# Sums of y's blocks on GpSimd beside the recurrence and memory attention, and both operands of the out-projection streamed, in a hybrid trunk layer on one core

## The chip, the cores and the metric

The kernel runs on one core of a Trainium2 chip. The metric is device time in microseconds (us), the median of several runs: 1556.83 us before the change, from 1556.57 to 1557.63 in three runs. Engines: TensorE (PE) multiplies matrices; VectorE (DVE), ScalarE (ACT) and GpSimd (POOL) work on elements; SyncE (SP) issues the DMAs of this kernel.

## The reference

One layer over 1024 rows of width 1024, in float32: a gated DeltaNet with 8 heads, a cross-attention of 4 heads over 256 memory tokens, one out-projection of both, and a SwiGLU FFN.

```python
def reference(x, mem, ...):
    h = x
    mem_n = rms_norm(mem, mem_norm)
    u = rms_norm(h, norm_pre_mix[layer])
    y_mix, q_mem = gdn_branch(u @ gdn_w_in[j], gdn_conv[j], gdn_a_log[j], gdn_dt_bias[j], gdn_out_norm[j])
    mem_k, mem_v = jnp.split(mem_n @ w_mem_kv[layer], 2, axis=-1)
    y_mem = memory_attention(q_mem, mem_k, mem_v)
    y = jnp.concatenate([y_mix, y_mem], axis=-1) @ w_out[layer]
    h = h + rms_norm(y, norm_post_mix[layer])
    f = swiglu(rms_norm(h, norm_pre_ffn[layer]), w_ffn_in[layer], w_ffn_out[layer])
    return h + rms_norm(f, norm_post_ffn[layer])

def memory_attention(q_mem, mem_k, mem_v):
    s = jnp.einsum("bhtd,bhmd->bhtm", q, k).astype(jnp.float32) * MEM_DH ** -0.5
    p = jax.nn.softmax(s, axis=-1).astype(v.dtype)
    return merge_heads(jnp.einsum("bhtm,bhmd->bhtd", p, v))
```

## The kernel before

All matrix products are float32 in three passes: each operand is split into a high part (a cast on ScalarE) and a low part (operand minus high part), and high x high, high x low and low x high are summed in PSUM. Who makes the low part depends on the place: here it is GpSimd for the left operand and VectorE for the right one.

The stages follow one another on TensorE, each filled up with products of the next: the input norm and transposes (to about 60 us); the recurrence over 8 heads in two halves of 512 rows, with the dense projections between its small products (to about 640); memory attention (to about 715); the out-projection (from 699 to about 854); the FFN's input products (to about 1317) and output products.

**Memory attention** has 16 units: 4 heads, two halves of the rows each, two units per half. `mem_q` projects a head's queries, `mem_scores` makes a unit's scores (psc), their maximum (mx), its negative scaled (nb), the exponential on ScalarE, its reciprocal sum (rc) and the product of both (pr). `mem_finish` takes the oldest unit from the list `pend`, transposes its probabilities (`mem_pt`, ptp) and, for the second unit of a half, multiplies by the values (`mem_pv`: pym, copied into ym and stored in y_d). Before the change a unit is finished after the scores of the next one, a lag of one. kvh and kvl are the halves of a head's keys and values.

**The out-projection** is y times w_out as 2 x 2 blocks. y has 12 heads of 128 columns: the first six columns of blocks (k = 0 to 5) belong to heads 0 to 5, the second six to heads 6 to 11, and its rows fall into two halves; these are A11, A12, A21, A22. Seven block products in Winograd's manner replace eight; `OPRODS` lists them for j = 0 to 6, and `o_prod(j)` runs one: six steps k, in each `o_operands(j, k)` loads and splits both operands (256 KB blocks), and `split_step` adds 4 x 3 matmuls, 72 for a product. The sums of w_out's blocks (T1 to T4) are made during the recurrence and stored in DRAM. The sums of y's blocks are made in the out-projection itself, in place in SBUF: in j = 1 A11 -= A21 (S3, VectorE) and A21 += A22 (S1, GpSimd), in j = 2 A22 -= A11 (S2, VectorE), in j = 3 A12 -= A22 (S4, VectorE), six adds each. So y's blocks stay in SBUF over the products, A11 and A12 in the pool `yp`, A21 and A22 in slots that belong to the FFN's weights (`free_slots`: names oB11h and so on in the trace). A22 itself is loaded again for j = 6, into the slots `raw` that the FFN's weights use too. `o_combine` adds a product's result to the output rows (hn<-acc).

Below, product 1 is j = 0, product 2 is j = 1, and so on. Beside the products VectorE and GpSimd also prepare the first weights of the FFN: multiply by a gain (L1057), sums of blocks (L1095), low parts (L93 for wlo<-raw, L1078 for plo and qlo).

Instructions go to an engine's queue in program order, except that `stage` and `issue_after` place a step behind a named instruction. An engine works its queue in order.

## Time and profile before

| | before |
|---|---|
| median of the runs shown | 1556.83 us |
| profiled execution | 1557.43 us |
| its span, first to last instruction | 1555.3 us |
| mean granted clock of TensorE | 0.986 |
| TensorE busy | 1477.7 us, 95% |
| VectorE busy | 1067.9 us, 69% |
| ScalarE busy | 680.4 us, 44% |
| GpSimd busy | 822.4 us, 53% |

The profile is of one execution; the times in its rows are measured from the span's start. The profiled execution took 2.1 us more than its span. A clock of 1.00 is TensorE's full speed (2.4 GHz), 0.50 its lower level (1.2 GHz).

### The profile page before, as it was taken

The page shows a single profiled execution, that of the slowest core. Times are in us where ns is not written, and L with a number is a line of the kernel's source. Part 1 is how long each engine was busy: PE and PEld are TensorE (multiplying, and loading weights), DVE is VectorE, ACT ScalarE, POOL GpSimd, SP SyncE. Part 2 cuts the span into 40 slices and gives each one's busy share as a digit, 9 for nine tenths or more (in the row PEclk, how much of TensorE's full clock was granted, in tenths as well). Part 3 has the DMA queues.
Part 4 walks back from the last instruction along what each step waited for, and adds up shares of the span by engine and source line. Part 5 has one row for each costly group of instructions (what it writes and reads, how often), then busy time and mean ns, then how long its engine had stood idle before and what let it go on. Part 6 is the DMA issues. An engine that isn't in the chain of part 4 may idle for free. (4 is left out here: it accounts for less than half of the span.)

```text
span 1555.3 us, 22654 instructions
## 1 busy us (share of the span) xinstructions
PE 1477.7 (95%) x8237; PEld 1180.3 (76%) x8237; DVE 1067.9 (69%) x1651; ACT 680.4 (44%) x1481; POOL 822.4 (53%) x705
## 2 busy tenths in 40 slices
PE   7999999999999999999898889999999999999996
PEld 5777777777777777887676668877887887778784
DVE  7565766656666757667977886666766766585967
ACT  7464445455454554345346532222222222544352
POOL 3543636464546544204755556666656565544455
PEclk9999999999999999999899899999999999999998
DMA  6411213122212220219334222222222324973334
GB/s 201 156 55 42 77 53 104 68 76 64 85 62 76 76 74 29 82 62 306 108 109 148 81 94 97 102 102 100 103 86 93 112 81 144 317 251 98 93 97 161
DMA packets 77554, 168.13 MB, mean 108 GB/s; under 512 B 10434, under 2 KB 12930, under 8 KB 77443
## 3 DMA queue, kind: packets, MB, share of 16 engines
q1 hardware_dynamic: 76720, 165.58, 31.9%
q8 instruction: 64, 1.05, 0.3%
q10 hardware_dynamic: 722, 1.12, 0.2%
q14 instruction: 48, 0.39, 0.1%
HBM read 124.42 MB, written 42.24 MB: 107 GB/s over the span
## 5 line engine op out<-in xcount | busy, mean ns | idle before, releaser
L246 PE MATMUL pj<-uhi,whi 128*128 128x512 f32 x496 | 215.7, 435 | 0.0
L93 POOL TENSOR_TENSOR wlo<-raw,whi 128x1024 fp32r<-128x1024 f32 x61 | 158.2, 2594 | 74.9 <-ACT whi L92 74.6
L246 PE MATMUL pj<-uhi,wlo 128*128 128x512 f32 x496 | 195.8, 395 | 0.0
L246 PE MATMUL pj<-ulo,whi 128*128 128x512 f32 x496 | 193.7, 391 | 0.0
L1292 POOL TENSOR_TENSOR wlo<-ar,whi 128x512 fp32r<-128x512 f32 x75 | 105.4, 1407 | 99.8 <-ACT whi L1291 99.8
L295 DVE SCALAR_TENSOR_TENSOR cv<-cb,convw_sb,cv 128x512 f32<-128x512 f32 x144 | 132.6, 921 | 24.0 <-ACT cv L290 23.3
L907 PE MATMUL fo<-wlo,whi 128*128 128x512 f32 x308 | 123.0, 399 | 9.4 <-DVE wlo L1292 9.2
L92 ACT CAST whi<-raw 128x1024 fp32r<-128x1024 f32 x66 | 69.6, 1055 | 119.2 <-DVE raw L1057 56.7
L908 PE MATMUL fo<-whi,wlo 128*128 128x512 f32 x308 | 120.6, 392 | 0.0
L906 PE MATMUL fo<-whi 128*128 128x512 f32 x308 | 118.4, 391 | 0.6 <-DVE c L854 0.6
L1095 DVE TENSOR_TENSOR raw<-raw 128x512 f32<-128x512 f32 x86 | 100.3, 1167 | 23.7 <-POOL wlo L93 13.7
L1292 DVE TENSOR_TENSOR wlo<-B,whi 128x512 fp32r<-128x512 f32 x75 | 80.9, 1081 | 45.9 <-ACT whi L1291 45.3
L246 PEld LDWEIGHTS pj<-uhi,wlo 128*128 128x128 f32 x496 | 93.1, 188 | 21.5 <-POOL wlo L93 0.2
L1057 DVE TENSOR_TENSOR raw<-raw,gcols_sb 128x1024 f32<-128x1024 f32 x44 | 64.1, 1457 | 57.9 <-DMA raw<-in_w_ffn_in 57.5
L246 PEld LDWEIGHTS pj<-ulo,whi 128*128 128x128 f32 x496 | 94.2, 190 | 10.8
L246 PEld LDWEIGHTS pj<-uhi,whi 128*128 128x128 f32 x496 | 94.0, 189 | 10.7 <-issue 0.2
L1291 ACT CAST whi<-ar 128x512 fp32r<-128x512 f32 x75 | 46.6, 621 | 113.1 <-POOL wlo L1292 75.4
L530 DVE TENSOR_TENSOR T<-pT,T 128x256 f16<-128x256 f32 x96 | 40.6, 423 | 59.5 <-PE pT L246 58.8
L907 PE MATMUL acc<-wlo,whi 128*128 128x512 f32 x168 | 68.7, 409 | 12.6 <-DVE wlo L891 12.6
L907 PEld LDWEIGHTS fo<-wlo,whi 128*128 128x128 f32 x308 | 58.2, 189 | 29.3 <-DVE wlo L1292 17.7
L1078 POOL TENSOR_TENSOR qlo<-raw,qhi 128x1024 fp32r<-128x1024 f32 x21 | 54.8, 2611 | 42.9 <-ACT qhi L1077 38.5
L517 DVE TENSOR_TENSOR zlev<-pz,lvmask_sb 128x256 f16<-128x256 f32 x96 | 40.4, 421 | 47.1 <-PE pz L246 47.0
(408 smaller groups left out, 4250.9 us busy)
## 6 DMA issues: line engine op xcount, KB each, us to landing
raw<-in_w_ffn_in SPq DMA_DIRECT2D x44, 512.0 KB, 3.3
raw<-in_w_in SPq DMA_DIRECT2D x36, 512.0 KB, 3.2
ar<-g_S SPq DMA_DIRECT2D x44, 256.0 KB, 2.6
B<-in_w_ffn_out SPq DMA_DIRECT2D x42, 256.0 KB, 4.6
g_A<-g SPq DMA_DIRECT2D x33, 256.0 KB, 2.0
ar<-g_A SPq DMA_DIRECT2D x29, 256.0 KB, 3.8
wsum<-in_w_out SPq DMA_DIRECT2D x24, 256.0 KB, 4.3
T_d<-wsum SPq DMA_DIRECT2D x24, 256.0 KB, 2.0
```

The costliest lines, as they stand in the source:

```text
L92: nc.scalar.copy(hi, raw)
L93: (lo_eng or nc.gpsimd).tensor_tensor(out=lo, in0=raw, in1=hi.bitcast(F32), op=ALU.subtract)
L246: ins = nc.tensor.matmul(*args, **kw)
L295: nc.vector.scalar_tensor_tensor(out=cf, in0=cb[:, c0:c0 + HF], scalar=w[:, j:j + 1], in1=cf, op0=ALU.mult, op1=ALU.add)
L906: nc.tensor.matmul(acc[n], hi[:, 0, ts_], hi[:, 1], start=first, stop=False)
L907: nc.tensor.matmul(acc[n], hi[:, 0, ts_], lo[:, 1], start=False, stop=False)
L908: return nc.tensor.matmul(acc[n], lo[:, 0, ts_], hi[:, 1], start=False, stop=last)
L1057: nc.vector.tensor_tensor(out=raw, in0=raw, in1=gcol[:, 1, :].unsqueeze(2).broadcast_to([P, ND, P]), op=ALU.mult)
L1078: nc.gpsimd.tensor_tensor(out=lo, in0=src, in1=hi.bitcast(F32), op=ALU.subtract)
L1095: nc.vector.tensor_tensor(out=o, in0=x, in1=y, op=op)
L1291: nc.scalar.copy(hi[:, i], src)
L1292: last_lo[i] = eng.tensor_tensor(out=lo[:, i], in0=src, in1=hi[:, i].bitcast(F32), op=ALU.subtract).ins
```

## The change

The six S3 = A11 - A21 are made on GpSimd in `post_y`, as each of heads 0 to 5 ends, and stored in DRAM (`s_d`). The other 18 sums (S2 = A22 - S3, S1 = A21 + A22, S4 = A12 - S2 for each k) are made on GpSimd by `y_sums`, in the loop over the units of memory attention: it loads A21 and S3, makes three sums and stores them. For k = 0 and 1 the second operands are heads 6 and 7, for k = 2 to 5 the fresh ym of a memory head. The out-projection holds no block: `o_operands` loads both operands of every step into the tags `oa` and `ob`, eight buffers each (the first two steps into `raw`). `o_sums`, `block` and `free_slots` are gone; j = 6 no longer uses `raw`. Memory attention finishes a unit after the scores of the second unit behind it, with three buffers for its small tiles.

```diff
@@ -46,8 +46,7 @@
 TFILL = (3, 4)
 W0 = 3
 POST = (1, 1, 2, 3)
-YP = ("A11", "A12")
-OPRODS = (("A11", "B11"), ("A12", "B21"), ("A22", "T2"), ("A21", "T1"), ("A12", "B22"), ("A11", "T3"),
+OPRODS = (("A11", "B11"), ("A12", "B21"), ("S2", "T2"), ("S1", "T1"), ("S4", "B22"), ("S3", "T3"),
           ("A22", "T4"))
 
 
@@ -67,6 +66,7 @@
     vm_d = [dram.tile([P, HF], F32, name=f"vm_d{i}") for i in range(2)]
     h_d = [dram.tile([P, D], F32, name=f"h_d{i}") for i in range(NT)]
     t_d = {n: [dram.tile([P, HF], F32, name=f"{n}_d{k}") for k in range(KH)] for n in ("T1", "T2", "T3", "T4")}
+    s_d = {n: [dram.tile([P, HF], F32, name=f"{n}_d{k}") for k in range(KH)] for n in ("S1", "S2", "S3", "S4")}
 
     def load_const(src, shape, dt, name, pool=None):
         t = (pool or const).tile(shape, dt, name=name)
@@ -631,13 +631,37 @@
         rstd_into(sc, rq2, 1.0 / (128.0 * 128.0), C4)
         nc.gpsimd.tensor_tensor(out=sc, in0=sc, in1=rq, op=ALU.mult)
         nc.gpsimd.tensor_scalar(out=sc, in0=sc, scalar1=128.0 ** -0.5, scalar2=1.0, op0=ALU.mult, op1=ALU.mult)
-        nc.gpsimd.tensor_tensor(out=os_, in0=os_, in1=bc(sc), op=ALU.mult)
+        st["os_ins"] = nc.gpsimd.tensor_tensor(out=os_, in0=os_, in1=bc(sc), op=ALU.mult).ins
 
     def post_y(h, hf, hd, st):
         pyt = transposes(st["os"], "pyt")
         y = hd["zs"][:, hf * HF:(hf + 1) * HF]
         nc.vector.scalar_tensor_tensor(out=y, in0=pyt, scalar=onorm, in1=y, op0=ALU.mult, op1=ALU.mult)
         nc.sync.dma_start(y_d[h][:, hf * HF:(hf + 1) * HF], y)
+        if hf == 1:
+            blocks = [hd["zs"][:, i * HF:(i + 1) * HF] for i in HO]
+            if h < KH:
+                t = pp.tile([P, HF], F32, tag="kvo", name="s3", bufs=3)
+                nc.gpsimd.tensor_tensor(out=t, in0=blocks[0], in1=blocks[1], op=ALU.subtract)
+                nc.sync.dma_start(s_d["S3"][h], t)
+            else:
+                ysums.append((h - KH, *blocks))
+
+    ysums = []
+
+    def y_sums(k, a12, a22):
+
+        s1 = hp.tile([P, HF], F32, tag="gr", name="s1", bufs=3)
+        nc.sync.dma_start(s1, y_d[k][:, HO[1] * HF:(HO[1] + 1) * HF])
+        s2 = hp.tile([P, HF], F32, tag="gr", name="s2", bufs=3)
+        nc.sync.dma_start(s2, s_d["S3"][k])
+        nc.gpsimd.tensor_tensor(out=s2, in0=a22, in1=s2, op=ALU.subtract)
+        nc.sync.dma_start(s_d["S2"][k], s2)
+        nc.gpsimd.tensor_tensor(out=s1, in0=s1, in1=a22, op=ALU.add)
+        nc.sync.dma_start(s_d["S1"][k], s1)
+        s4 = hp.tile([P, HF], F32, tag="gr", name="s4", bufs=3)
+        nc.gpsimd.tensor_tensor(out=s4, in0=a12, in1=s2, op=ALU.subtract)
+        nc.sync.dma_start(s_d["S4"][k], s4)
 
     def wo_block(i, j, k):
 
@@ -771,16 +795,16 @@
             nc.tensor.matmul(o, qh[:, t0:t0 + P], kvh[:, :NM], start=True, stop=False)
             nc.tensor.matmul(o, qh[:, t0:t0 + P], kvl[:, :NM], start=False, stop=False)
             nc.tensor.matmul(o, ql[:, t0:t0 + P], kvh[:, :NM], start=False, stop=True)
-        mx2 = small.tile([P, 2], F32, tag="mx2", name="mx2")
+        mx2 = small.tile([P, 2], F32, tag="mx2", name="mx2", bufs=3)
         nc.vector.tensor_reduce(out=mx2, in_=psc.rearrange("p (j m) -> p j m", j=2), axis=AX.X, op=ALU.max)
-        nb = small.tile([P, 2], F32, tag="nb", name="nb")
+        nb = small.tile([P, 2], F32, tag="nb", name="nb", bufs=3)
         nc.vector.tensor_scalar(out=nb, in0=mx2, scalar1=-MEM_SCALE, scalar2=None, op0=ALU.mult)
         pr = hp.tile([P, 2, NM], F32, tag="E", name="pr", bufs=3)
-        sm = small.tile([P, 2], F32, tag="sm", name="sm")
+        sm = small.tile([P, 2], F32, tag="sm", name="sm", bufs=3)
         for j in range(2):
             nc.scalar.activation(pr[:, j, :], psc[:, j * NM:(j + 1) * NM], AF.Exp,
                                  bias=nb[:, j:j + 1], scale=MEM_SCALE, accum_out=sm[:, j:j + 1])
-        rc = small.tile([P, 2], F32, tag="rc", name="rc")
+        rc = small.tile([P, 2], F32, tag="rc", name="rc", bufs=3)
         nc.vector.reciprocal(rc, sm)
         for j in range(2):
             nc.vector.tensor_scalar(out=pr[:, j, :], in0=pr[:, j, :], scalar1=rc[:, j:j + 1],
@@ -803,9 +827,15 @@
         for m in range(2):
             c0 = NM + m * P
             mm3(py, kvh[:, c0:c0 + P], kvl[:, c0:c0 + P], pth[m], ptl[m], m == 0, m == 1)
-        ym = hp.tile([P, HF], F32, tag="os", name="ym", bufs=2)
+        ym = hp.tile([P, HF], F32, tag=("os", "uf")[hm % 2], name="ym", bufs=2)
         nc.vector.tensor_copy(ym, py)
         nc.sync.dma_start(y_d[H + hm][:, hf * HF:(hf + 1) * HF], ym)
+        yms.append(ym)
+        if len(yms) == 2:
+            ysums.append((hm + H - KH, *yms))
+            yms.clear()
+
+    yms = []
 
     def mem_units():
         for hm in range(MH):
@@ -832,18 +862,22 @@
             with tc.issue_after(pj_ins[0]):
                 stage(post_y, ypend.pop(i))
         pend.append((hf, n2, cur, tiles, mem_scores(hf, n2, *cur)))
-        if len(pend) > 1:
+        if len(pend) > 2:
             mem_finish()
+        if i >= 4 and i % 2 == 0 and ysums:
+            with tc.issue_after(st[2 * H - 1]["os_ins"]):
+                y_sums(*ysums.pop(0))
     mem_finish()
+    mem_finish()
+    for job in ysums:
+        y_sums(*job)
     s1u.close()
-
 
 
 
 
     s2y = ExitStack()
     yp = s2y.enter_context(tc.tile_pool(name="yp", bufs=1, reuse_waits="tile"))
-    oblk = {}
 
     def load_row(pool, i):
         t = pool.tile([P, D], F32, name=f"grow{i}", bufs=1)
@@ -854,7 +888,9 @@
         return eng.tensor_tensor(out=out, in0=x, in1=y, op=op)
 
     def load_block(t, name, k):
-        if name[0] == "A":
+        if name[0] == "S":
+            src = s_d[name][k]
+        elif name[0] == "A":
             i, j = int(name[1]) - 1, int(name[2]) - 1
             src = y_d[k + KH * j][:, HO[i] * HF:(HO[i] + 1) * HF]
         else:
@@ -864,27 +900,14 @@
     def o_raw():
         return wp.tile([P, 2, HF], F32, tag="raw", name="raw", bufs=2)
 
-    def block(name, k):
-        if (name, k) not in oblk:
-            t = yp.tile([P, HF], F32, name=f"{name}_{k}", bufs=1) if name in YP else free_slots.pop(0)
-            oblk[name, k] = t
-            load_block(t, name, k)
-        return oblk[name, k]
-
     def o_operands(j, k):
-        an, bn = OPRODS[j]
-        first = j == 0 and k < 2
-        raw = o_raw() if j == 6 or first else None
-        if j == 2:
-
-            add(block("A22", k), block("A22", k), block("A11", k), op=ALU.subtract)
-        if raw is None:
-            srcs = [block(an, k)]
+        if j == 0 and k < 2:
+            raw = o_raw()
+            srcs = [raw[:, 0], raw[:, 1]]
         else:
-            srcs = [raw[:, 0]]
-            load_block(raw[:, 0], an, k)
-        srcs.append(raw[:, 1] if first else yp.tile([P, HF], F32, tag="ob", name="ob", bufs=OB))
-        load_block(srcs[1], bn, k)
+            srcs = [yp.tile([P, HF], F32, tag=t, name=t, bufs=OB) for t in ("oa", "ob")]
+        for src, name in zip(srcs, OPRODS[j]):
+            load_block(src, name, k)
         hi, lo = (wp.tile([P, 2, HF], F32R, tag="w" + c, name="w" + c, bufs=3) for c in ("hi", "lo"))
         for i, (src, eng) in enumerate(zip(srcs, (nc.gpsimd, nc.vector))):
             nc.scalar.copy(hi[:, i], src)
@@ -892,14 +915,6 @@
         return hi, lo
 
     last_lo = [None, None]
-
-    def o_sums(j, k):
-
-        if j == 1:
-            add(block("A11", k), block("A11", k), block("A21", k), op=ALU.subtract)
-            add(block("A21", k), block("A21", k), block("A22", k), nc.gpsimd)
-        elif j == 3:
-            add(block("A12", k), block("A12", k), block("A22", k), op=ALU.subtract)
 
     def split_step(acc, n, first, last, hi, lo):
         ts_ = slice(n * P, (n + 1) * P)
@@ -1010,7 +1025,6 @@
         for k in range(KH):
             hl = o_operands(j, k)
             with tc.issue_after(last_lo[0]), tc.issue_after(last_lo[1]):
-                o_sums(j, k)
                 if j and k < 4:
                     o_combine(j - 1, k, oprev[0][k])
                 if j >= 5:
@@ -1124,11 +1138,6 @@
     bp = s4.enter_context(tc.tile_pool(name="bp", bufs=1, side="right", reuse_waits="tile"))
     s2 = ExitStack()
     pt_ = s2.enter_context(tc.tile_pool(name="pt", bufs=2, side="right", reuse_waits="tile"))
-    free_slots = []
-    for pool, tags, n in ((bp, ("B11h", "B11l", "B21h", "B21l"), 4), (mp, ("phi", "plo", "qhi", "qlo"), 2)):
-        for tag in tags:
-            t = pool.tile([P, n, HF], F32, tag=tag, name="o" + tag, bufs=1)
-            free_slots += [t[:, i] for i in range(n)]
     x1, x2 = ([pt_.tile([P, D], F32, tag="hn", name="hn", bufs=8) for _ in range(4)] for _ in range(2))
     grow = {0: load_row(pt_, 0)}
     wx = s2y.enter_context(tc.tile_pool(name="wx", bufs=1, reuse_waits="tile"))
```

On VectorE, from the second product on (the numbers behind A_0 to A_5 and acc are those of tiles; A_0_8805 and its like are blocks A11, oB11h and its like blocks A21 and A22). Before:

```order
L854 TENSOR_TENSOR A_0_8805<-A_0_8805,oB11h 128x512
L891 TENSOR_TENSOR wlo<-ob,whi 128x512
L854 TENSOR_TENSOR A_1_8834<-A_1_8834,oB11h 128x512
L854 TENSOR_TENSOR oB11h<-oB11h,A_0_8805 128x512
L854 TENSOR_TENSOR A_2_8671<-A_2_8671,oB11l 128x512
L854 TENSOR_TENSOR oB11h<-oB11h,A_1_8834 128x512
L891 TENSOR_TENSOR wlo<-ob,whi 128x512
L854 TENSOR_TENSOR A_3_8693<-A_3_8693,oB11l 128x512
L854 TENSOR_TENSOR oB11l<-oB11l,A_2_8671 128x512
L854 TENSOR_TENSOR A_4_8715<-A_4_8715,oB21h 128x512
L854 TENSOR_TENSOR oB11l<-oB11l,A_3_8693 128x512
L891 TENSOR_TENSOR wlo<-ob,whi 128x512
```

After, from the second product's first low parts to the middle of the third (hn<-acc_8891 is the first sum with a result of product 2):

```order
L914 TENSOR_TENSOR wlo<-ob,whi 128x512 x7
L1071 TENSOR_TENSOR raw<-raw,gcols_sb 128x1024
L888 TENSOR_TENSOR hn<-acc_8891,hn 128x512
L914 TENSOR_TENSOR wlo<-ob,whi 128x512
L888 TENSOR_TENSOR hn<-acc_8892,hn 128x512
L1071 TENSOR_TENSOR raw<-raw,gcols_sb 128x1024
L1109 TENSOR_TENSOR raw<-raw 128x512
L914 TENSOR_TENSOR wlo<-ob,whi 128x512
L888 TENSOR_TENSOR hn<-acc_8893,hn 128x512
L1109 TENSOR_TENSOR raw<-raw 128x512
L1109 TENSOR_TENSOR s_9193<-raw 128x512
L1109 TENSOR_TENSOR raw<-raw,s_9193 128x512
```

The sums between the low parts are gone, and so are both multiplies between them (L1071, L1057 before): one stood in the second product and now stands at the start of the third, where the other one, the sums of FFN weights (L1109, L1095 before) and hn stood already.

On GpSimd, from the second product on, before (oB11h<-oB11h and its like are the sums S1; wlo<-A are low parts of the second product, wlo<-oB11h of the third):

```order
L891 TENSOR_TENSOR wlo<-A_0_8795,whi 128x512
L891 TENSOR_TENSOR wlo<-A_1_8824,whi 128x512
L891 TENSOR_TENSOR wlo<-A_2_8853,whi 128x512
L93 TENSOR_TENSOR wlo<-raw,whi 128x1024
L854 TENSOR_TENSOR oB11h<-oB11h 128x512
L891 TENSOR_TENSOR wlo<-A_3_8880,whi 128x512
L854 TENSOR_TENSOR oB11h<-oB11h 128x512
L891 TENSOR_TENSOR wlo<-A_4_8907,whi 128x512
L854 TENSOR_TENSOR oB11l<-oB11l 128x512 x2
L891 TENSOR_TENSOR wlo<-A_5_8933,whi 128x512
L854 TENSOR_TENSOR oB21h<-oB21h 128x512 x2
L891 TENSOR_TENSOR wlo<-oB11h,whi 128x512 x2
```

After, from the low parts of the first product's last three steps (the rows with s and ym are the last group of sums, for k = 5):

```order
L914 TENSOR_TENSOR wlo<-oa,whi 128x512 x3
L658 TENSOR_TENSOR s_8720<-ym,s_8720 128x512
L660 TENSOR_TENSOR s_8718<-s_8718,ym 128x512
L663 TENSOR_TENSOR s_8726<-ym,s_8720 128x512
L914 TENSOR_TENSOR wlo<-oa,whi 128x512 x8
L93 TENSOR_TENSOR wlo<-raw,whi 128x1024
L914 TENSOR_TENSOR wlo<-oa,whi 128x512 x2
L1092 TENSOR_TENSOR plo<-raw,phi 128x512
L1092 TENSOR_TENSOR plo<-s_9193,phi 128x512
L1092 TENSOR_TENSOR qlo<-raw,qhi 128x1024
L914 TENSOR_TENSOR wlo<-oa,whi 128x512 x16
```

The last group of sums stands between the low parts of the first and the second product, and L93 has moved behind eight low parts, which is into the third product, ahead of plo and qlo (L1078 before).

On GpSimd in the recurrence, after (L645 is the new S3, between the work of two heads; nothing else in these rows is new):

```order
L85 TENSOR_TENSOR rk<-rs,mhalf 128x4
L283 MEMSET cb 128x4
L645 TENSOR_TENSOR s_4510<-zs 128x512
L629 TENSOR_TENSOR rq_4533<-rq_4533,ss_4497 128x4
L83 TENSOR_SCALAR rs<-rq_4533 128x4
L85 TENSOR_TENSOR sc<-rs,mhalf 128x4
```

The subtraction stands behind a head's last small work and ahead of the next head's L629.

## Rows read from the trace of the kernel before

**Rows 1.** The page, busy time of each engine, share of the span, instructions.

```profile
PE 1477.7 (95%) x8237; PEld 1180.3 (76%) x8237; DVE 1067.9 (69%) x1651; ACT 680.4 (44%) x1481; POOL 822.4 (53%) x705
```

**Rows 2.** Windows: us, busy by engine, instructions; then clock, DMA share, GB/s.

```profile
640.00:720.00 80.00, 78.83 (x419) 63.17 (x418) 53.62 (x139) 42.05 (x129) 13.03 (x13) 1.00 0.36 120
726.00:750.00 24.00, 19.80 (x74) 14.97 (x74) 21.78 (x18) 8.76 (x16) 19.24 (x12) 0.86 0.66 228
750.00:774.00 24.00, 19.51 (x76) 14.73 (x75) 21.98 (x20) 11.40 (x23) 18.19 (x11) 0.93 0.38 121
790.00:806.00 16.00, 16.00 (x73) 13.23 (x72) 10.01 (x11) 7.56 (x14) 7.81 (x6) 1.00 0.34 99
806.00:830.00 24.00, 17.68 (x75) 13.53 (x74) 20.24 (x19) 13.53 (x27) 19.42 (x24) 1.00 0.43 155
```

**Rows 3.** TensorE's waits from 726 to 774: total us, times, longest.

```profile
PE acc L907 <- DVE wlo L891: 7.5, 4, 2.8
PE acc L908 <- POOL wlo L891: 1.2, 2, 0.6
```

**Rows 4.** Timeline of TensorE: start, duration, instruction, idle time before it.

```profile
750.17 0.39 PE L906 MATMUL acc<-whi 128*128 128x512 f32 x1
753.35 0.50 PE L907 MATMUL acc<-wlo,whi 128*128 128x512 f32 x1 [2.78 <-DVE wlo L891]
...
754.92 0.63 PE L906 MATMUL acc<-whi 128*128 128x512 f32 x1
...
757.48 0.48 PE L906 MATMUL acc<-whi 128*128 128x512 f32 x1
757.80 0.40 PE L907 MATMUL acc<-wlo,whi 128*128 128x512 f32 x1
758.03 0.39 PE L908 MATMUL acc<-whi,wlo 128*128 128x512 f32 x1
```

**Rows 5.** Timeline of VectorE in the second and third product.

```profile
736.05 1.77 DVE L854 TENSOR_TENSOR A<-A,oB11l 128x512 f32<-128x512 f32 x1
...
741.12 0.68 DVE L854 TENSOR_TENSOR A<-A,oB11l 128x512 f32<-128x512 f32 x1
...
751.54 1.75 DVE L891 TENSOR_TENSOR wlo<-ob,whi 128x512 fp32r<-128x512 f32 x1
```

**Rows 6.** Timeline of GpSimd in the first three products.

```profile
717.13 1.30 POOL L891 TENSOR_TENSOR wlo<-A,whi 128x512 fp32r<-128x512 f32 x1 [4.57 <-ACT whi L890]
...
737.23 1.75 POOL L891 TENSOR_TENSOR wlo<-A,whi 128x512 fp32r<-128x512 f32 x1
...
764.50 2.41 POOL L1078 TENSOR_TENSOR qlo<-raw,qhi 128x1024 fp32r<-128x1024 f32 x1
```

**Rows 7.** VectorE's groups, 726 to 774: count, busy us, mean ns, idle before.

```profile
L854 DVE TENSOR_TENSOR hn<-acc,hn 128x512 f32<-128x512 f32 x5 | 3.4, 678 | 0.0
L1057 DVE TENSOR_TENSOR raw<-raw,gcols_sb 128x1024 f32<-128x1024 f32 x2 | 2.4, 1211 | 0.0
...
L1095 DVE TENSOR_TENSOR raw<-raw,s 128x512 f32<-128x512 f32 x1 | 0.7, 695 | 0.0
```

**Rows 8.** VectorE's groups in memory attention, 640 to 726.

```profile
L777 DVE TENSOR_SCALAR nb<-mx 128x2 f32<-128x2 f32 x16 | 4.3, 276 | 0.0
...
L757 DVE TENSOR_TENSOR kvl<-kvr,kvh 128x512 fp32r<-128x512 f32 x3 | 2.0, 682 | 0.0
```

**Rows 9.** Timelines of VectorE and GpSimd at 711.

```profile
711.48 1.11 DVE L777 TENSOR_SCALAR nb<-mx 128x2 f32<-128x2 f32 x1
...
711.27 1.30 POOL L891 TENSOR_TENSOR wlo<-A,whi 128x512 fp32r<-128x512 f32 x1 [5.35 <-DVE mx L775]
```

**Rows 10.** The window with the most DMA traffic around the products.

```profile
720.00:740.00 20.00, 17.84 (x78) 14.12 (x76) 15.51 (x12) 10.88 (x19) 14.31 (x9) 1.00 0.94 334
```

**Rows 11.** Timeline of GpSimd in the recurrence.

```profile
395.07 0.64 POOL L484 TENSOR_SCALAR_AFFINE_SELECT at<-at 128x512 f32<-128x512 f32 x1 [2.86 <-DVE at L481]
```

## The prediction

> **What bounds the kernel now.** The page's busy times come first: TensorE works 1477.7 of 1555.3 us, VectorE 69%, GpSimd 53% [rows 1]. A gain has to come out of the 78 us that TensorE idles, or out of work at a low clock. Next, the windows: in memory attention TensorE is busy 78.83 of 80 us, in the fifth product 16.00 of 16; in products 2 and 3 it is busy 19.80 and 19.51 of 24 us, at granted clocks of 0.86 and 0.93 [rows 2]. A product is 72 matmuls. At the pace of 790 to 806 (73 records in 16 us, 0.219 us each, those cut by the edges counted in) 24 us would hold 109.5; the two windows hold 74 and 76. So product 2 loses 35.5 x 0.219 = 7.8 us and product 3 33.5 x 0.219 = 7.3. Product 6 (806 to 830, 75 records) loses about as much, but no sum stands there.
>
> The waits of these 48 us name VectorE's wlo (7.5 us) and GpSimd's (1.2) [rows 3]. What delays them is in the engines' own order. On VectorE an add of two SBUF tiles takes 0.68 us at 741.12 and 1.77 at 736.05 [rows 5]; GpSimd's multiplies of the same size take 1.30 at 717.13, with VectorE elsewhere, and 1.75 at 737.23 [rows 6]. At 733 to 741 both engines are full with sums and wlo, and each prolongs the other. VectorE's hn<-acc, with one operand from PSUM, keeps its 0.68 us through the same stretch [rows 7]. So it is not the number of sums alone that costs, but two-SBUF work of both engines at once: each has to wait out the other's instruction.
>
> **The change part by part.**
>
> *Sums leave products 2 and 3.* Gone are 12 VectorE adds and 6 GpSimd adds from product 2 and the start of 3, and 6 VectorE adds from product 4 (no loss there, so 0). Product 2 then holds no more than wlo of both engines, 6 x (0.68 + 1.30) = 11.9 us of two-SBUF work in 16.3, less than product 5, which also loses nothing: I take off its whole loss, -7.8. Product 3 opens with a wait: one matmul at 750.17, the next at 753.35, 3.18 us less a pace of 0.23, or 2.95 [rows 4], for the wlo that starts at 751.54 and takes 1.75 us, behind the last sum on VectorE [rows 5]. Behind that wait TensorE runs at the lower level (1.2 GHz): from 754.92 to 757.48 six matmuls take 0.427 each, just after 0.23 again; that is 1.2 us, and I add 0.4 for the matmuls on both sides of them, 1.6 [rows 4]. Both leave with the sums: -2.95 - 1.6 = -4.55. Removed together: -12.35.
>
> *What stays in product 3, and gets more.* Of its 7.3, 7.3 - 4.55 = 2.75 belong to the preparation of the FFN weights. The order shows that GpSimd's 128x1024 lo (L93), which stood in product 2, now stands in product 3 among the wlo, ahead of the two plo and the qlo, and VectorE's first multiply (L1057) moves from product 2 to the start of 3. They take 2.4, as the qlo of the same size does [rows 6], and 1.2 us [rows 7]. If they find room, 0; if all of it reaches TensorE, +3.6; I take half, +1.8, since product 3 is already the fuller one.
>
> *The 18 sums beside memory attention.* They are three GpSimd instructions for each k, some 1.3 us each, 4 to 5 us a group. GpSimd is nearly empty there (13.03 of 80 us [rows 2]), so their own time is hidden; the price is what they do to VectorE, busy 53.62 of these 80 us. The only neighbours in the trace: nb, a tiny VectorE operation, takes 1.11 us at 711.48 while a GpSimd wlo runs from 711.27 to 712.57 [rows 9], and 0.16 otherwise (the mean of 16, 276 ns, holds two such hits [rows 8]). A hit thus costs 1.11 - 0.16 = 0.95. Bounds: 0, if the lag of two covers all, to 18 x 0.95 = 17.1, if every sum hits a chain that TensorE waits for. TensorE waits for the softmax chain only after two more units, about 5 us each (16 units in 80 us), so hits on nb or pr vanish; not covered is the change of heads, where kvl and the copy into ym stand directly ahead of TensorE's next products [rows 8]. A group starts just after the second ym of a head, thus exactly there. Five groups with one hit each, some 0.6 of its 0.95 seen by TensorE: +3.0. That is nearer to the low end, since 5 of 18 sums are exposed.
>
> *The last group and the start of product 2.* On GpSimd the last three sums wait for the last ym, and all wlo of product 2 stand behind them. That ym ends at about 720.8 (before the change); three sums give 724.7 to 725.9 (1.30 to 1.7 each), the first wlo 726.0 to 727.6. Product 2's third matmul, which reads it, is due at 726.7. The wlo that follow need 1.3 to 1.75 per step of 2.7, so the delay doesn't return. From 0 to +4 (a later ym by the lag, contention on every instruction); taken +0.5.
>
> *S3 in the recurrence.* Six GpSimd subtractions of 1.3 us. GpSimd waits there for VectorE (2.86 us before the select at 395.07 [rows 11]). They are hidden in those waits; without this cover 6 x 1.3 = 7.8. Taken +0.5.
>
> *The lag of two.* It can give back no more than what memory attention loses: 80 - 78.83 = 1.2 [rows 2]. Bounds -1.2 and 0; taken half, -0.6. The extra buffers take no instruction.
>
> *Streamed operands.* A product now loads 12 blocks of 256 KB, 3.1 MB in 16.3 us or 193 GB/s; the core has moved 334 GB/s in 720 to 740 [rows 10], without a wait for a DMA in the products. On SP the stores of the last group stand ahead of product 3's first loads: free at about 726, wanted at about 740. 0. The second FFN load no longer waits for raw slots that product 7 held; that can only help products 6 and 7: 0 to -6, taken 0.
>
> The sum: -12.35 + 1.8 + 3.0 + 0.5 + 0.5 - 0.6 = -7.15. The profiled execution took 1557.43, which gives 1550.3; the median is 0.6 lower, so **1549.7 us**, 0.5% less.
>
> The Trainium skill, page "SBUF — State Buffer", section "Who interferes with whom", speaks against this change: VectorE and GpSimd share a port pair that one instruction holds to its end, two SBUF operands or VectorE's two-port modes (copy, tensor_scalar) take it, and one SBUF operand at most doesn't. The rows agree: 0.68 against 1.77 us for an add, 0.68 throughout for hn<-acc [rows 5, 7]. Its rule is rival A below.
>
> **The rivals.**
> *A. GpSimd's sums hold up VectorE in memory attention, slower (10%).* Mechanism: each sum runs against pr, nb, kvl; VectorE, two thirds busy, falls behind by one hit per sum, and the lag doesn't refill. For it: the hit at 711.48 [rows 9]. Against it: VectorE has 26 us of idle in the 80 [rows 2], 18 hits take 17. At full price 17.1 + 7.8 for the S3 hits instead of 3.5: 1549.7 + 21.4 = 1571. The break-even is 18 sums at 0.56 us seen by TensorE each (7.15 + 3.0 = 10.15 over 18); by this case the time is 1560 to 1571. By the page's rule, tensor_scalar pr would be hit as well, which makes this case's 17.1 and no more.
> *B. Product 3 stays as slow as it is (25%).* Without sums it still holds 6 x 1.98 = 11.9 us of wlo, and 2.4 (L93) + 2 x 1.3 (plo) + 2.4 (qlo) on GpSimd and 2 x 1.2 (L1057) + 4 x 0.69 (L1095) on VectorE [rows 6, 7]: 24.5 us of two-SBUF work in 16.3. If the two engines exclude each other fully, 8.2 us are lost, less what wlo's three buffers run ahead. For it: that sum, and that product 5, with 11.9, loses nothing. Against it: product 2 runs light, so product 3 starts some steps ahead. Loss 8.2 in place of 2.75 + 1.8: 1549.7 + 3.6 = 1553.3, and 1552 to 1554 with what the lead is worth and the start of product 2 costs.
> *C. Product 6 and what follows gain too (12%).* Product 6 loses 24 - 75 x 0.219 = 7.6 us [rows 2], through FFN weights prepared beside it. If those of the next k are loaded and multiplied in memory attention, half of it goes: 1549.7 - 5 = 1545. Against it: the order of VectorE's and GpSimd's rows from product 4 on is the old one.
> *D. Nothing comes of it (8%).* The streams are late: 42 loads and 24 new stores on one queue, and product 3 reads S2 that was stored 15 us earlier. The wait on VectorE becomes one for a DMA of about the same size: 1556 to 1557. Against it [rows 10].
>
> **How the numbers follow.** The forecast itself has 45%, its own range 1546 to 1552. B gives 1552 to 1554, C 1542 to 1546, D about 1557, A 1560 and more. A measurement here tells about 0.2%, 3.1 us, from no change: faster is below 1553.7. The forecast, C and two thirds of B lie there: 0.73; D and the rest of B are the same: 0.17; A is slower: 0.10. The range from 1540 to 1557 leaves out A and a little below C.
>
> **What would show it.** In the profile after: product 2 in about 16.5 us with TensorE's clock at 1.0 in it, no wait for VectorE's wlo above 1 us; product 3 in 20 to 21.5 us, with a wait for GpSimd's wlo behind L93 or qlo (at 24 B holds). VectorE's nb and kvl of 1 us and more beside s<-ym in memory attention, yet TensorE's gaps there some 3 us in sum (10 or more: A). First matmul of product 2 with no wait over 0.5 us. No wait for oa or ob anywhere. Wrong I'd be most easily in the 3.0 for memory attention and in product 3's rest.

## The result and the profile after

The changed kernel takes 1564.92 us (median of 9 runs, 1561.69 to 1566.86), the kernel before 1557.32 (9 runs, 1549.87 to 1562.69): ratio 1.0052, 95% interval 1.0031 to 1.0072. It is slower by half a per cent, and clear of the noise, where 0.5% less was forecast. The profiled execution took 1561.69, its span is 1559.9 us.

Executions of one and the same kernel differ by some 20 us (25 runs of the kernel before beside experiment 1 took 1547.71 to 1568.79). So the comparisons below go by single stretches of TensorE's order: the start of one named matmul to that of another, read from the timelines, one profiled execution of each kernel.

| stretch, us | before | after | difference |
|---|---|---|---|
| recurrence: first pkk of unit 3 to first pkk of unit 15 | 422.4 | 431.5 | +9.1 |
| rest of it, memory attention, product 1 | 123.6 | 129.2 | +5.6 |
| product 2 | 23.9 | 17.1 | -6.8 |
| product 3 | 23.6 | 23.4 | -0.2 |
| products 4 and 5 | 32.6 | 32.6 | 0.0 |
| products 6 and 7 | 47.4 | 45.7 | -1.7 |
| sum | 673.5 | 679.4 | +6.0 |

(pkk are the products of a unit's keys; a product runs from its first matmul to the next product's first, and the last row ends at the start of product 7's last matmul; differences and sum are from the unrounded numbers.) Busy times on the page after, against [rows 1]:

```profile
PE 1482.8 (95%) x8237; PEld 1177.5 (75%) x8237; DVE 1047.8 (67%) x1633; ACT 679.7 (44%) x1481; POOL 845.5 (54%) x723
```

VectorE has 18 instructions less and GpSimd 18 more, as planned; TensorE, with the same 8237 records, is busy 5.1 us longer, a first hint that its work itself has become slower somewhere. The windows that answer to [rows 2]: memory attention (the same 80 us from the span's start, though the work comes some 10 us later now), product 2, product 3, product 5, product 6.

```profile
640.00:720.00 80.00, 75.59 (x413) 60.66 (x412) 50.16 (x124) 35.66 (x112) 31.43 (x30) 1.00 0.46 151
742.00:759.00 17.00, 16.53 (x74) 13.36 (x73) 8.37 (x8) 9.27 (x17) 10.40 (x8) 1.00 0.97 340
759.00:783.00 24.00, 19.43 (x77) 14.64 (x76) 19.75 (x18) 11.68 (x25) 19.03 (x11) 0.93 0.63 204
799.00:815.00 16.00, 16.00 (x73) 13.23 (x72) 9.95 (x11) 7.57 (x14) 7.77 (x6) 1.00 0.61 197
815.00:840.00 25.00, 19.52 (x74) 14.38 (x73) 19.49 (x19) 14.60 (x27) 20.35 (x24) 0.94 0.56 189
```

Product 2 is cured: 17 us, clock 1.00, while DMA moves 340 GB/s. Product 3 is what it was, clock 0.93 and all.

**The recurrence.** TensorE's waits from unit 3 to unit 15, before and then after:

```profile
PE pc L246 <- DVE vn L597: 3.9, 13, 0.3
```

```profile
PE pc L246 <- DVE vn L597: 8.3, 18, 1.0
```

Five more waits of just under 1 us, one for each of the first five S3; the sixth, made at 599.5 near the end of the stretch, has none. The timeline of GpSimd after, at one of them, shows an S3 and what stands behind it:

```profile
382.03 1.29 POOL L645 TENSOR_TENSOR s<-zs 128x512 f32<-128x512 f32 x1 [9.72 <-DVE zs L639]
383.28 0.20 POOL L629 TENSOR_TENSOR rq<-rq,ss 128x4 f32<-128x4 f32 x1
...
387.37 1.04 POOL L457 TENSOR_TENSOR E<-gr,gc 128x512 f32<-128x512 f32 x1
388.36 1.49 POOL L634 TENSOR_TENSOR os<-os,sc 128x512 f32<-128x512 f32 x1
389.81 1.09 POOL L458 TENSOR_SCALAR_AFFINE_SELECT E<-E 128x512 f32<-128x512 f32 x1
```

The S3 hides in nothing: the 9.72 us ahead of it are its own wait for zs, and when zs comes, everything behind it is due. E ends at 390.9. The timelines of ScalarE (first before, then after), VectorE and TensorE carry it on:

```profile
384.50 0.63 ACT L469 ACTIVATE E<-E 128x512 f32<-128x512 f32 x1 [0.48 <-POOL E L458]
```

```profile
390.93 0.63 ACT L469 ACTIVATE E<-E 128x512 f32<-128x512 f32 x1 [1.77 <-POOL E L458]
...
394.40 0.69 ACT L290 ACTIVATE cv<-pj,convw_sb 128x512 f32<-128x512 f32 x1
```

```profile
395.19 0.75 DVE L295 SCALAR_TENSOR_TENSOR cv<-cb,convw_sb,cv 128x512 f32<-128x512 f32 x1 [1.50 <-ACT cv L290]
...
396.20 0.34 DVE L597 TENSOR_SCALAR vn<-pc,beta 128x128 f32<-128x128 f32 x1
```

```profile
396.59 0.49 PE L246 MATMUL pc<-vn,kg 128*128 128x128 f32 x2 [0.97 <-DVE vn L597]
```

ScalarE's exponential waits for E (1.77 us; before, at the same place, 0.48), the convolution's scaling stands behind it in ScalarE's queue, the taps wait for that on VectorE, and vn stands behind the taps. None of these engines is full; the delay goes through the heads of four queues.

**Memory attention.** At the second head, VectorE and then TensorE:

```profile
677.35 0.68 DVE L781 TENSOR_TENSOR kvl<-kvr,kvh 128x512 fp32r<-128x512 f32 x1
679.94 1.77 DVE L1071 TENSOR_TENSOR raw<-raw,gcols_sb 128x1024 f32<-128x1024 f32 x1 [1.91 <-DMA raw<-in_w_ffn_in]
681.63 1.27 DVE L799 TENSOR_REDUCE mx<-psc 128x2 f32<-128x512 f32 x2
```

```profile
684.15 0.39 PE L795 MATMUL psc<-kvh,qh 128*128 128x256 f32 x1 [2.28 <-ACT pr L805]
```

An FFN weight's multiply has moved here, because product 7 no longer holds the raw slots. It waits for its load, then runs beside a GpSimd sum, and the maxima stand behind it. In the last head the sums hit kvl and a low part of product 1 (0.68 us each when alone):

```profile
718.04 0.93 DVE L781 TENSOR_TENSOR kvl<-kvr,kvh 128x512 fp32r<-128x512 f32 x1 [1.02 <-DMA ob<-in_w_out]
718.89 1.77 DVE L914 TENSOR_TENSOR wlo<-ob,whi 128x512 fp32r<-128x512 f32 x1
```

The nb that the prediction priced is not hit (0.15 to 0.23 us, all 16).

**Product 3**, VectorE after:

```profile
760.71 2.83 DVE L1071 TENSOR_TENSOR raw<-raw,gcols_sb 128x1024 f32<-128x1024 f32 x1
763.64 1.59 DVE L1109 TENSOR_TENSOR raw<-raw 128x512 f32<-128x512 f32 x1
765.16 1.75 DVE L914 TENSOR_TENSOR wlo<-ob,whi 128x512 fp32r<-128x512 f32 x1
```

The multiply that takes 1.2 us in [rows 7] takes 2.83 beside GpSimd's L93 and wlo. The wait at the product's start is gone; TensorE now waits further on (total, times, longest, from 759 to 783):

```profile
PE acc L922 <- DVE wlo L914: 4.0, 2, 2.3
```

### The profile page after: what moved, and what is told of

Its sections match the earlier page's. It is cut to its first block, busy times and chain, and to the rows that moved or that the text cites. A ratio compares the mean times of both kernels' runs of the same rounds, so it can differ in the third digit from the quotient of the medians.

```text
span 1559.9 us, 22814 instructions
## 1 busy us (share of the span) xinstructions
PE 1482.8 (95%) x8237; PEld 1177.5 (75%) x8237; DVE 1047.8 (67%) x1633; ACT 679.7 (44%) x1481; POOL 845.5 (54%) x723
## 5 line engine op out<-in xcount | busy, mean ns | idle before, releaser
L93 POOL TENSOR_TENSOR wlo<-raw,whi 128x1024 fp32r<-128x1024 f32 x61 | 156.8, 2571 | 74.9 <-ACT whi L92 74.7
L295 DVE SCALAR_TENSOR_TENSOR cv<-cb,convw_sb,cv 128x512 f32<-128x512 f32 x144 | 139.4, 968 | 30.0 <-ACT cv L290 29.3
L1109 DVE TENSOR_TENSOR raw<-raw 128x512 f32<-128x512 f32 x86 | 102.8, 1195 | 24.5 <-POOL wlo L93 15.2
L246 PEld LDWEIGHTS pj<-uhi,whi 128*128 128x128 f32 x496 | 93.9, 189 | 11.8 <-issue 0.2
L1071 DVE TENSOR_TENSOR raw<-raw,gcols_sb 128x1024 f32<-128x1024 f32 x44 | 61.8, 1404 | 60.3 <-DMA raw<-in_w_ffn_in 59.7
L914 POOL TENSOR_TENSOR wlo<-oa,whi 128x512 fp32r<-128x512 f32 x40 | 57.2, 1437 | 51.2 <-ACT whi L913 45.9
```

The lines of the kernel that those rows point to most:

```text
L93: (lo_eng or nc.gpsimd).tensor_tensor(out=lo, in0=raw, in1=hi.bitcast(F32), op=ALU.subtract)
L246: ins = nc.tensor.matmul(*args, **kw)
L295: nc.vector.scalar_tensor_tensor(out=cf, in0=cb[:, c0:c0 + HF], scalar=w[:, j:j + 1], in1=cf, op0=ALU.mult, op1=ALU.add)
L914: last_lo[i] = eng.tensor_tensor(out=lo[:, i], in0=src, in1=hi[:, i].bitcast(F32), op=ALU.subtract).ins
L1071: nc.vector.tensor_tensor(out=raw, in0=raw, in1=gcol[:, 1, :].unsqueeze(2).broadcast_to([P, ND, P]), op=ALU.mult)
L1109: nc.vector.tensor_tensor(out=o, in0=x, in1=y, op=op)
```

## The experiments

All times of stretches are as in the table above; "memory attention" is its second line. Ratios are against the kernel before, run beside each. How far one stretch can differ from profile to profile shows in experiment 6: up to product 3 it works as the changed kernel does, yet its memory attention took 130.9 us against 129.2. Differences there of less than 1.7 us say little.

**1. S3 alone.** The kernel before, and in `post_y`:

```diff
+        if hf == 1 and h < KH:
+            blocks = [hd["zs"][:, i * HF:(i + 1) * HF] for i in HO]
+            t = pp.tile([P, HF], F32, tag="kvo", name="s3", bufs=3)
+            nc.gpsimd.tensor_tensor(out=t, in0=blocks[0], in1=blocks[1], op=ALU.subtract)
+            nc.sync.dma_start(s_d["S3"][h], t)
```

> The kernel before, with nothing added but the six S3 = A11 - A21 on GpSimd in the recurrence, at the place that the change gives them, and their stores; the result is not used. Theory 1 (each S3 stands on GpSimd ahead of the next unit's E; E feeds ScalarE's exponential, ScalarE's queue holds the convolution's copy behind it, VectorE's taps come late and with them vn, for which TensorE waits): 1.4 us for each of six heads, the first score product of memory attention 8 to 9 us later, the time 7 to 9.5 us above before. Rival 1 (S3 hides in GpSimd's waits, and the lateness comes from other parts of the change): within 2 us of before.

Recurrence 429.3, 7.0 us above before; TensorE's waits there:

```profile
PE pc L247 <- DVE vn L598: 9.5, 18, 1.1
```

So theory 1 holds for the stretch. The whole time did not show it: 1557.73 us, ratio 1.0017 (0.9982 to 1.0051), a miss of the expected 7 to 9.5, though the interval still holds 7 us. Its profiled execution had 454.3 us in the FFN's input products, with code like that of before, which took 463.6 there. That is the spread told of above, and a reason to go by stretches.

**2. S3 behind al.** The changed kernel, with

```diff
+        if s3s and i % 2 == 1:
+            with tc.issue_after(st[i]["al_ins"]):
+                s3_sum(*s3s.pop())
         if i % 2 == 1 and 1 <= h <= KH:
```

> The changed kernel, with each S3 issued on GpSimd behind the low part al of the next unit instead of ahead of that unit's post and E. The same 1.3 us of GpSimd, another place. Theory 1 (the place ahead of E costs): 7 to 9 us less than the changed kernel, TensorE's wait for vn back to about 5 us from 9.4. Rival 2 (GpSimd has no 1.3 us to spare in a head, wherever they stand): at most 2 us less.

1576.81 us, ratio 1.0123 (1.0071 to 1.0176); recurrence 443.8, 12.4 us worse still. Both expectations missed. The wait for vn is 5.0 us, so the old chain is free; another has taken its place:

```profile
PE pz L246 <- DVE T L530: 11.5, 7, 2.2
```

(1.6 us, 2 times, before.) S3 here stands ahead of rk and of the sums of w_out's blocks, whose buffers (tag kvo) it shares; GpSimd waits 35.0 us for their loads instead of some 14. Which of the two delays T was not traced.

**3. A lag of one.** The changed kernel with `len(pend) > 1`.

> The changed kernel with memory attention's lag of one unit again. If the lag of two covers what GpSimd's sums do to VectorE there, this is 3 to 6 us slower than the changed kernel. If the lag is worth no more than the idle time that was there before (1.2 us), within 1.5 us of it either way. If the lag itself costs (psc tiles held longer), 1 to 3 us faster.

1560.8 us, 1.0021 (0.9997 to 1.0046); memory attention 129.1 against 129.2. With the sums on GpSimd the lag is worth nothing in this stretch, nor does it cost.

**4. The 18 sums without their arithmetic.** In `y_sums` the three GpSimd instructions are left out and the operands stored.

> The changed kernel, leaving out the arithmetic of the 18 sums beside memory attention (S1, S2 and S4 are stored as the bare operands; all loads and stores stay, S3 stays). Theory 2 (GpSimd's two-SBUF work prolongs VectorE's there, and that is what memory attention and the first product lost, some 7 us): 5 to 7 us less than the changed kernel. Rival 3 (the loss is the FFN weight's multiply that has moved into memory attention, with its wait for a DMA ahead of the maxima on VectorE): at most 2 us less, and TensorE's gap of 2.3 us at the second head stays.

1562.59 us, 1.0033 (1.0003 to 1.0063); memory attention 125.6, 3.6 us less, product 2 16.3 instead of 17.1. That lies between the two expectations: the arithmetic is two thirds of what memory attention lost. The gap at the second head, which rival 3 expected to stay, is gone as well: the multiply still stands there, but waits for nothing and takes 1.22 us.

**5. S3 behind the sums of w_out's blocks.** As 2, with `s3_sum` behind `weight_sums`, so that three of its four sums stand ahead of S3.

> The changed kernel, with each S3 on GpSimd behind al and three of the four sums of w_out's blocks of the next unit, ahead of a stretch of some 10 us in which GpSimd waits for ScalarE (rq <- junk). Theory 1, narrowed (GpSimd has the time in a head, but ahead of E as in the change, or ahead of rk as with S3 behind al alone, an S3 delays a chain that TensorE waits for): the recurrence, from the kernel products of unit 3 to those of unit 15, takes 422 to 425 us against 431.5, the time is 6 to 9 us less than the changed kernel's. Rival 2 (no room on GpSimd anywhere in a head): 431 us or more.

1557.79 us, 1.0017 (0.998 to 1.0054); recurrence 425.5, 5.9 us less, TensorE's waits:

```profile
PE pc L246 <- DVE vn L597: 3.5, 13, 0.3
```

The place was the cost: GpSimd does the same work here for nothing (experiment 10 has the same time without it). But 3.1 us above before remain with no wait to show for them, and memory attention took 133.2, 4.0 more than after; that was not traced.

**6. The FFN weights' preparation spread.**

```diff
         if j == W0:
-            gate_w(0)
-            up_w(0)
+            with tc.issue_after(last_lo[0]), tc.issue_after(last_lo[1]):
+                gate_w(0)
+        if j == W0 + 1:
+            with tc.issue_after(last_lo[0]), tc.issue_after(last_lo[1]):
+                up_w(0)
```

> The changed kernel, with the preparation of the first FFN weights held back: the first weight's behind product 3's low parts, the second's behind product 4's. Theory 3 (product 3 lost 7 us to two-SBUF work of both engines, 24.5 us of it in 16.3): product 3 takes 16.3 to 17 us against 23.4, products 4 and 5 at most 18 each, since each gets only a part; 5 us less in sum over the three. Rival 4 (the loss goes with the preparation, wherever it stands): products 4 and 5 together 6 to 7 us longer than 32.6.

Windows of product 3 and product 5:

```profile
762.00:778.50 16.50, 16.50 (x74) 13.67 (x73) 9.69 (x11) 9.74 (x19) 9.77 (x7) 1.00 0.85 281
794.90:814.00 19.10, 16.98 (x74) 13.37 (x73) 13.46 (x14) 8.89 (x16) 15.59 (x11) 1.00 0.57 176
```

Product 3 takes 16.3 us at full clock, product 4 16.4, product 5 19.1, beyond the expected 18: 4.2 us less over the three. Theory 3 holds in so far as the loss left product 3 with the work; the second part is still too much for one product. The edit also puts the work behind the product's low parts in both queues; whether the amount or the place of it counts was not separated. One run, 1567.07 us, 467.6 of it in the FFN's input products.

**7. The second FFN weight's multiply held back.** `gate_w(1)` under `issue_after` of product 7's last low parts.

> The changed kernel, with the second FFN weight's multiply on VectorE, which had moved into memory attention, held back behind the out-projection. It stood there ahead of the maxima mx and waited 1.9 us for its DMA, then took 1.8 us. If that is what memory attention lost beside the sums: TensorE's gap of 2.3 us at the second head goes, and memory attention with product 1 is 2 to 2.6 us shorter than in the changed kernel. If the maxima would have been late by GpSimd's sums anyway: at most 1 us.

The gap at the second head is gone, and memory attention proper is 2.3 us shorter up to product 1's first matmul (57.1 against 59.4), but product 1 is 1.8 longer: 128.6 against 129.2 in all, 0.6, which is within the spread told of above. One run, 1566.35 us. The gap goes without the multiply as it goes without the sums (experiment 4), but of the two only the sums show in the whole stretch.

**8. Edits 5, 6 and 7 together.**

> The changed kernel with the three edits together: S3 behind the sums of w_out's blocks, the first FFN weights' preparation spread over products 4 and 5, the second weight's multiply behind the out-projection. If theories 1 and 3 hold and the parts add: 8.5 + 5 + 2.3 = about 16 us less than the changed kernel, some 1549, 8 us below before, in a measurement that can tell 4. If the FFN's first products then wait for the weight prepared late: half of it.

1554.65 us, 0.9984 (0.9957 to 1.0011): the loss is undone, no gain is left. Recurrence 425.4, memory attention 129.0, product 3 16.3. From unit 3 to the end of product 7 it takes 668.9 us against 679.4, so 10.5 of the expected 16 us came. Against the 673.5 of before it is 4.6 less, which the whole times cannot tell from nothing.

**9. The 18 sums on VectorE.** `nc.vector` for `nc.gpsimd` in `y_sums`.

> The changed kernel with the 18 sums beside memory attention on VectorE, at the same places, instead of GpSimd; S3 stays on GpSimd. If GpSimd's instructions cost there by prolonging VectorE's two-SBUF work (theory 2): an add takes 0.68 us on VectorE, 12 us in sum into 26 us of idle, and memory attention with product 1 is 2 to 4 us shorter than in the changed kernel (129.2 us from the last kernel product to product 2). If VectorE's order is what costs (a sum that waits for its load holds up the maxima behind it): 2 to 6 us longer.

Memory attention 126.6, 2.6 us less, as theory 2 expected; product 2 16.3. One run, 1554.62 us. Every profile of the change with these sums on GpSimd has 128.6 us or more in memory attention, the three without (experiments 4, 9 and 12) 126.6 or less. On VectorE an uncontended sum is 0.69 us:

```profile
L663 DVE TENSOR_TENSOR s<-ym,s 128x512 f32<-128x512 f32 x4 | 2.7, 685 | 0.0
```

**10. All sums beside memory attention.** Edit 8, with S3 as a fourth sum in `y_sums`.

> The version with the three edits together, and S3 too beside memory attention on GpSimd (four sums for each k there, six more in all; S4 is made in place), nothing of the sums in the recurrence. The recurrence back to 422.4 us from 425.4, since no S3 stands in it. Memory attention with product 1: if each sum costs what the 18 cost (3.7 us without against with their arithmetic, 0.2 us each), 1.2 us more; in sum 2 us less than the three edits, about 1552. If four sums in a row hold up the low parts of product 1 behind them: 3 us more or worse, no gain.

1555.64 us, 0.9999 (0.997 to 1.0028); memory attention 130.4, 1.4 more than in 8, as expected. But the recurrence, now with no S3 in it, is 425.4, the same as in 8. So S3 costs nothing at the place of 5, and the 3 us are something else. They grow by a quarter of a microsecond per unit, in steps too small to be a wait: a matmul pj<-ulo,whi is followed by the next after 233.4 ns (mean of the back-to-back pairs from 185 to 600 us), 228.3 before.

**11. The small tiles' third buffer alone.** The kernel before, and four times

```diff
-        nb = small.tile([P, 2], F32, tag="nb", name="nb")
+        nb = small.tile([P, 2], F32, tag="nb", name="nb", bufs=3)
```

> The kernel before with nothing changed but the third buffer for memory attention's four small tiles (mx2, nb, sm, rc), 32 bytes more per partition in a pool that is allocated ahead of the projections' operands. Open: the recurrence of every version with the change takes 425.4 us or more from the kernel products of unit 3 to those of unit 15, 3 us more than before, even with no S3 in it, in the same order on TensorE, and a projection's matmul starts every 233.3 ns behind one by ulo, against 228.3. Theory 5 (the operands' places in SBUF have moved by these 32 bytes, and the matmuls read them slower): 425.4 us here and 233 ns. Rival 6 (the additional traffic or work of the change slows them): 422.4 us and 228 ns.

Recurrence 425.3. The page's group of these matmuls (count, busy us, mean ns), in the order before, after, this one, and the next experiment:

```profile
L246 PE MATMUL pj<-ulo,whi 128*128 128x512 f32 x496 | 193.7, 391 | 0.0
```

```profile
L246 PE MATMUL pj<-ulo,whi 128*128 128x512 f32 x496 | 195.9, 395 | 0.0
```

```profile
L246 PE MATMUL pj<-ulo,whi 128*128 128x512 f32 x496 | 195.9, 395 | 0.0
```

```profile
L246 PE MATMUL pj<-ulo,whi 128*128 128x512 f32 x496 | 193.7, 391 | 0.0
```

Four tiles of 8 bytes, not one instruction more, the same order on TensorE, and the whole 3 us are there (one run, 1562.2 us). What the buffers moved can be read from the built program: each takes a slot of 32 bytes per partition, so uhi and ulo, the high and low part of u, which the projections' matmuls stream past the weights, lie 128 bytes further on, not 32 (ulo0 at 87840 before, at 87968 here); whi and wlo of these products lie where they lay. The pace follows it in every profile: 228.3 to 228.6 ns in the three with two buffers (before, experiments 1 and 12), 233.3 to 233.4 in the eleven with three, on several chips and with a granted clock of 1.00 in the stretch.

**12. The best of these.** Edit 8, two buffers for the small tiles and a lag of one, the 18 sums on VectorE.

> The version with the three edits, with two buffers for the small tiles and a lag of one again, and with the 18 sums beside memory attention on VectorE. If theory 5 holds: the recurrence back to 422.4 us (3 less than the three edits). If the sums cost less on VectorE, as they did alone (2.6 us less up to product 2, 0.8 in product 2): together 6 us less than the three edits, about 1548, and 8 below before. Rival: 425.4 us in the recurrence still, and VectorE's sums, with the lag of one, hold up the softmax: no gain on the three edits.

1546.65 us (11 runs) against 1559.67 (16 runs of the kernel before): ratio 0.9919, 0.9887 to 0.9952, faster by 0.8%. Recurrence 422.4, as theory 5 expected, memory attention 125.4, products 2 to 4:

```profile
731.00:747.00 16.00, 16.00 (x72) 13.27 (x71) 8.71 (x8) 9.44 (x18) 7.86 (x7) 1.00 0.97 343
747.00:764.00 17.00, 17.00 (x77) 14.03 (x76) 10.18 (x11) 9.81 (x20) 10.27 (x7) 1.00 0.84 275
764.00:780.00 16.00, 16.00 (x73) 13.23 (x72) 13.62 (x15) 7.48 (x14) 9.02 (x7) 1.00 0.67 202
```

From unit 3 to the end of product 7: 661.6 us, 17.8 less than after and 11.8 less than before. The change's idea, with the 18 sums on VectorE, and the spread preparation together are good for that much; what the spreading alone would have given the kernel before was not tried.

## Why the prediction was wrong

*Product 2* (forecast -7.8, and +0.5 for a wait at its start): right, -6.8; 17.1 us are 0.8 above the full pace of 16.3, which lies at its start. With the sums on VectorE or their arithmetic left out the product takes 16.3 us.

*S3 in the recurrence* (forecast +0.5): the step that failed. I read one wait of GpSimd, 2.86 us at [rows 11], as cover for an instruction that stands elsewhere. The wait is behind E's chain, S3 ahead of it: the 1.29 us of an S3 delay E, and through the queues of ScalarE and VectorE the vn that TensorE waits for. S3 cost 6 to 7 us (experiments 1 and 5), next to the bound of 7.8 "without this cover". The prediction didn't name what is queued behind S3, nor who waits for that.

*The lag of two* (forecast -0.6, "the extra buffers take no instruction"): they take none, and cost 3.0 us by moving uhi and ulo (experiments 11 and 12), a term that stood at nothing. No row of before could have shown it. The lag itself gave nothing (129.2 us with it, 129.1 without).

*Memory attention* (forecast +3.0, less 0.6 for the lag): about the right size for the sums (3.6 by experiment 4), too small for the whole, +5.6. The size was luck in part: the prediction priced it by hits on nb, and none came; pr, kvl, the multiply and product 1's low parts were hit. Of the other 2.0 us 0.4 appears in experiment 11 too and 0.6 goes with the multiply (experiment 7), both less than the spread; what they are stays open. The streams' case C saw only the good side of raw slots that come free: what starts sooner also stands in somebody's way.

*Product 3* (forecast -4.55 + 1.8): rival B, which had 25%. Its first wait went, and two-SBUF work (instructions of VectorE and GpSimd with two operands in SBUF) filled the room; experiment 6 took the work away, and the 7 us with it. The sum of both engines' two-SBUF work against the 16.3 us of a product is a better guide here than either engine's share. Counted is what runs between a product's first matmul and the next one's, at the durations without contention (0.68, 1.2, 1.30 and 2.4 us): 11.9 us (product 5) lost nothing, nor did 14.0 and 15.8 (products 3 and 4 of experiment 6); 18.4 (its product 5) lost 2.8, and 23.9 (product 3 of the changed kernel) lost 7.1. Rival B's 24.5 has one multiply too many: the first of the two runs in product 2's time, as it did before, so it did not move into product 3 as the prediction read the order. These are five points; that the sum alone decides is not shown.

*Streamed operands* (forecast 0) held: TensorE has no wait for oa or ob, with up to 340 GB/s moved. *Products 6 and 7* (forecast 0): -1.7, but experiment 1, with the out-projection of before, has 45.7 us there too, and experiment 6, with that of the change, 47.2, so this isn't the change's. (Rival C takes off 5 us for half of 7.6, which is 3.8; nothing else rests on it.)

In sum, over the stretch of the table: forecast -7.15, measured +6.0. Of the 13.1 us between them 8.6 are the recurrence (S3's place 6 and the layout 3, less the 0.5 forecast), 3.2 memory attention, 2.5 product 3, 0.5 product 2, less 1.7 in products 6 and 7. Rival A (GpSimd's sums hold up VectorE in memory attention) came out on the right side, and in its range of 1560 to 1571, by luck: its 17.1 us of hits were 3.6, and the S3 that it charged with 7.8 cost their 6 by their place in the queue.

The Trainium skill, page "SBUF — State Buffer", section "Who interferes with whom", says that a VectorE instruction with two SBUF inputs contends with a GpSimd instruction that reads SBUF, and that tensor_scalar can contend as well. The rows agree with it: the multiply takes 1.2 us alone and 2.83 beside GpSimd's work, and pr, a tensor_scalar, at most 0.36 us in memory attention before, where GpSimd is nearly idle, and up to 1.39 after. The rule bears on product 3 and on memory attention; the 6 us of S3 went away with its place in the queue.

## What to carry to other kernels

An idle engine is room only at the place in its queue where it idles: before an instruction is put there, follow what stands behind it through the other engines' queues to the one that bounds, and put it behind the last such instruction. Where two engines share work of two SBUF operands, add up both engines' share in each stage, and spread it before moving it. When a stretch gets slower with no wait in it, compare the starts of its bare matmuls: a change of buffers in a pool that is allocated ahead of the operands moves them.

## What the runs showed of the hardware

With uhi and ulo 128 bytes further on in each partition, and the weights where they were, matmuls of 128x512 float32r start their successors later (experiment 11 against before, back-to-back pairs from 185 to 600 us): 233.3 ns instead of 228.3 behind one by ulo, 234.4 instead of 231.6 behind uhi,whi, 235.3 instead of 234.2 behind uhi,wlo. Together that cost 3.0 us over the 420 us of the recurrence; with the old places (experiment 12) it is 228.3 again. Which of the two operands counts, and which places are good, was not tried.

The FFN's input products took from 454.3 to 467.6 us in the profiles of these kernels, whose TensorE instructions there are the same but for the order of a few transposes. TensorE's wait for GpSimd's qlo in that stretch, in the kernel before and in experiment 1 (total, times, longest):

```profile
PE sc L137 <- POOL qlo L1078: 10.8, 7, 3.5
```

```profile
PE sc L138 <- POOL qlo L1084: 3.5, 1, 3.5
```

What decides between one such wait and seven stays open.
